# A streaming-encoder block on one core: when a merged row is squared, where one half of a gate is kept, and how the last norm is fed and cut

## The chip, the core and the metric

The kernel runs on one core of a Trainium2 chip. The metric is the time of one execution in microseconds (us), as the device reports it; lower is better. In the profile the engines are called PE (TensorE, with PEld for its loads of stationary weights), DVE (VectorE), ACT (ScalarE), POOL (GpSimd) and SP (SyncE, which here only issues DMAs). ACT and POOL issue some DMAs too, and each engine works through its own instructions strictly in program order.

## What is computed

One layer over a sequence of 1024 tokens with 1024 channels, in float32 at its edges:

```python
x = x + 0.5 * swiglu_ffn(rms_norm(x, ffn1_norm), ffn1_w_in, ffn1_w_out)
h = rms_norm(x, mix_norm)
q_a, k_a, v_a, q_i, k_i, w_i, u_s, q_m, gates = split(h @ w_in)
o_a = indexed_sparse_attention(q_a, k_a, v_a, q_i, k_i, w_i, rel_bias) @ w_o_a
y_s = gelu(s5_layer(u_s, ...))
glu_a, glu_b = split(y_s @ w_glu, 2)
o_b = glu_a * sigmoid(glu_b)
o_m = memory_attention(q_m, m_k, m_v) @ w_o_m
g = sigmoid(gates)                                   # three gates per channel
merged = g[:, :, 0] * o_a + g[:, :, 1] * o_b + g[:, :, 2] * o_m
x = x + merged @ w_out
x = x + 0.5 * swiglu_ffn(rms_norm(x, ffn2_norm), ffn2_w_in, ffn2_w_out)
x = rms_norm(x, final_norm)
```

The change touches the place where `merged` is formed, and the last `rms_norm`.

## The kernel before

**Layout.** Activations are kept transposed: 128 channels on the partitions, tokens along the free axis. A "row" is one such slab of 128 channels by 1024 tokens, so there are 8 rows (d = 0 to 7), and a row has two halves of 512 tokens. Each float32 operand of a matrix product is split into two float16 parts, high and low, and a product is three matmuls (high by high, high by low, low by high). Before a row can be an operand it is scaled by a power of two taken from its sum of squares.

**Order of the work.** The program is laid out by hand-written generators (threads) that a small planner interleaves: a cost model keeps a clock for each engine and decides which thread takes its next step, and after each step it issues, ahead of time, preparation of the weight blocks that come next (load, squares, scale, high part, low part), as long as its model says that ACT and DVE are less than 3 us behind PE. The planner only fixes the program order; on the chip each engine runs its list and waits on semaphores.

**The merging loop** (in `mixer`) has 16 steps, n = 2d + half. A step does 30 matmuls into four PSUM banks: `gb` (the GLU's second half), `ga` (its first half), `pm` (memory attention) and `po` (sparse attention); `ga` and `po` take turns in the two banks called mm. The other engines then merge. ACT evaluates `sb` = tanh(gb), `gc` = a scaled copy of ga, and `sm` = a scaled copy of pm; DVE multiplies them with each other and with the three gates, which come back from DRAM through a GpSimd DMA (`g_in`, 768 KB a step) into a ring of three places in the big buffer `xa`; POOL adds sb and sm. The last part of a step, `rest`, belongs to `po`, and is issued at the head of the next step: ACT copies po to the row's place `m` in `xa`, DVE multiplies it with its gate, POOL adds sb. `sb`, `sm` and `gc` come from one ring of four temporary places (`t2`).

When the second half of a row is done, `rest` also calls `w["m"].put(d, ...)`. That starts the row's split, in three parts: first ACT squares the row (with the sum); then, at the next `w["m"].more()`, DVE makes the scale by two operations on one column (and two more for the inverse), and ACT writes the high part; at the `more()` after that DVE writes the low part. A step calls `more()` twice, ahead of the loads of gates and after POOL's first add.

**After the loop** comes the product with `w_out` (`out_stage`). Its first weight block, `w["out"][0]`, is scaled by factors of the rows 0 to 5, so its scale can only be made when row 5 is split: a weighted sum on DVE (`wj`), a matmul with ones on PE, three or four small operations on DVE, and then high and low part of each of the six pieces on ACT and DVE. `w["out"][0].go(("split", 0))` at the end of the loop issues whatever the planner has not issued by then. Four output pieces run their part over rows 0 to 5 before rows 6 and 7 are needed.

**The end of the kernel.** The second FFN's output product (`out_stage` again) adds to `x`; `final` turns each finished piece back to tokens by channels with PE transposes (`turn`), multiplies it with the norm's weights `gb` (broadcast to all partitions, in a place of `xa` that the FFN's gate rows used), and with the last channel row works out the token's rstd and scales and stores the finished tokens. The last output piece (d = 7, second half) is cut into two pieces of 256 tokens, by `cut=(0, HT // 2, HT)`. `gb` is loaded by a DMA on ACT's queue just before this stage's loads of `x`.

Of the kernel before, what the change touches and what calls it, by code (L numbers as in the profile page):

```python
# [17 lines left out]
P = 128  # L18
S = 1024
D = 1024  # L20
ND = D // P
HT = 512
# [582 lines left out]
class Builder:  # L605
# [1605 lines left out]
    def mixer(self, w, xa, ss, xd_in, xd_out, after):  # L2211


        nc, tc, sched = self.nc, self.tc, self.sched
# [84 lines left out]
        heads = lambda t, half: lambda i, k: t[:, 4 * half:4 * half + 4, 2 * k + i]  # L2299
        gates, mt, xf = {}, {}, xa.rearrange("p k a h t -> p (k a h t)")  # L2300
        room = lambda i, n: xf[:, i * HT:(i + n) * HT].rearrange("p (j t) -> p j t", j=n)

        def g_in(n):
            if n < 2 * ND:
# [7 lines left out]
        for n in range(2 * ND):  # L2312
            d, half = divmod(n, 2)
            b = w["go"][d // 2]
            glu, wm, wa = b.segs
            c = (d % 2) * P
            yield from self.stream.begin(b)
            gb, ga = self.bank("lg"), self.mm()
            self.matmul3(gb, lambda i, k: glu.hl[:, i, k, 256 + c:256 + c + P], w["y"].x(half), 2)
            if late:  # L2320
                late.pop()()
            yield None
            self.matmul3(ga, lambda i, k: glu.hl[:, i, k, c:c + P], w["y"].x(half), 2)
            sb, sm, gc = self.t2("sb"), self.t2("sm"), self.t2("gc")
            nc.scalar.activation(sb, gb, AF.Tanh, scale=glu.inv)
            yield None
            w["m"].more()
            g_in(n + 2)
            ta, tg, tm = (gates[n][:, j] for j in range(3))
            pm, po = self.bank("ao"), self.mm()  # L2330
            self.matmul3(pm, lambda i, k: wm.hl[:, i, k, c:c + P], heads(qmS, half), 2)
            nc.scalar.activation(gc, ga, AF.Copy, scale=glu.inv)
            nc.vector.scalar_tensor_tensor(sb, sb, 1.0, gc, op0=OP.add, op1=OP.mult)
            nc.vector.scalar_tensor_tensor(sb, tg, 1.0, sb, op0=OP.add, op1=OP.mult)
            yield None
            self.matmul3(po, lambda i, k: wa.hl[:, i, k, c:c + P], heads(qS, half), 4, ks=range(2))
            nc.scalar.activation(sm, pm, AF.Copy, scale=wm.inv)
            nc.vector.scalar_tensor_tensor(sm, tm, 1.0, sm, op0=OP.add, op1=OP.mult)
            nc.gpsimd.tensor_tensor(sb, sb, sm, op=OP.add)
            w["m"].more()  # L2340
            yield None
            self.matmul3(po, lambda i, k: wa.hl[:, i, k, c:c + P], heads(qS, half), 4, ks=range(2, 4))
            self.stream.end(b)
            if half == 0:
                mt[d] = room(9 + 2 * (d % 3), 2)

            def rest(d=d, half=half, wa=wa, po=po, ta=ta, sb=sb):
                m = mt[d][:, half]
                nc.scalar.activation(m, po, AF.Copy, scale=wa.inv)
                nc.vector.scalar_tensor_tensor(m, ta, 1.0, m, op0=OP.add, op1=OP.mult)  # L2350
                nc.gpsimd.tensor_tensor(m, m, sb, op=OP.add)
                if half == 1:
                    w["m"].put(d, mt[d].rearrange("p h t -> p (h t)"))

            late.append(rest)
            yield None
        w["out"][0].go(("split", 0))
        late.pop()()
        self.stream.BACKLOG = 3
        nc.free.add(xa.tensor.name)  # L2360
        en.close()
        xo, F = after()
        pool = m3.enter_context(tc.tile_pool(name="xo4", bufs=1, side="right"))
        xo = xo + [pool.tile([P, HT], F32, name="xo4", tag=f"xo4{i}") for i in range(3)]
        xo = iter([xo[i % len(xo)] for i in range(2 * ND)])
# [54 lines left out]
def tile_hybrid_block(ctx, tc, x, mem, ffn1_norm, ffn1_w_in, ffn1_w_out, mix_norm, w_in, a_q_gain, a_k_gain, rel_bias,  # L2420
# [66 lines left out]
    def main():  # L2487
        yield from kb.ffn_in("1", pa, a1, g1, xa, before)
        for h in range(2):
            sched.add(kb.norm_split(xa, h, lambda h=h: kb.row_sums(ss[h]), 1, "2"), 0)  # L2490
        xo = lambda: pa.tile([P, 2, HT], F32, name="xo", tag="gt", bufs=2)[:, 0]
        yield from kb.out_stage(b1, g1, xo, xd[0], 1, 2, kb.keep_x("2", xa, ss, xd[1]))
        st.close()
        with ExitStack() as en:
            F = {}

            def after():
                pool = en.enter_context(tc.tile_pool(name="g3", bufs=1, reuse_waits="tile"))
                F["pool"], F["B12", 0] = pool, pool.tile([P, ND // 2, 2, HT // 2], F16, name="FB12", tag="wsum1")
                names = ("B11", "B21", "B22", "T1", "T2", "T3", "T4")  # L2500
                F["all"] = pool.tile([P, len(names), ND // 2, 2, HT], F16, name="F")
                for i, n in enumerate(names):
                    F[n] = F["all"][:, i]
                F["xo"] = [pool.tile([P, HT], F32, name="xo3", tag=f"xo3{i}") for i in range(4)]
                return F["xo"], F

            yield from kb.mixer(mw, xa, ss, xd[1], xd[2], after)
            nc.free.discard(xa.tensor.name)
            pool = en.enter_context(tc.tile_pool(name="g4", bufs=1, reuse_waits="tile"))
            F["B12", 1] = pool.tile([P, ND // 2, 2, HT // 2], F16, name="FB12", tag="H7")  # L2510
            tiles = xa.rearrange("p k a h t -> p (k a h t)").rearrange("p (i t) -> p i t", t=HT)
            n = {"post": 0, "gt": 0, "xo": 0}

            def ring(kind):
                n[kind] += 1
                i = n[kind] - 1
                if kind == "xo":
                    return F["xo"][i % 4]
                if kind == "gt":
                    i = 8 + 2 * (i % 2)  # L2520
                    return tiles[:, i:i + 2].rearrange("p i t -> p (i t)")
                return tiles[:, i % 8]

            def room(k):
                k %= chunks[0][1]
                if k > 8:
                    i = 12 + 2 * (k - 9)
                    return tiles[:, i:i + 2].rearrange("p i t -> p (i t)").bitcast(F16).rearrange("p (j t) -> p j t", j=2)
                return pool.tile([P, 2, S], F16, name="H", tag=f"H{k}")

            g2.room = room
            early = lambda f: pool.tile([P, 2 * HT], F32, name="early", tag=f"H{4 + f}")
            yield from kb.ffn_strassen("3", g2, a2, b2, F, ring, early, chunks, xd[2])
            gb = tiles[:, 8:10].rearrange("p i t -> p (i t)")
            nc.scalar.dma_start(gb, final_norm.to_broadcast([P, D]))
            xt = F["all"].rearrange("p n k j t -> p (n k j t)").bitcast(F32)[:, 0:S * D // P].rearrange("p (i n) -> p i n", n=D)
            done, between = kb.final(xt, ss, gb, out[0])
            yield from kb.out_stage(b2[-1], g2, lambda: ring("xo"), xd[2], 2, 2, done, 3, cut=(0, HT // 2, HT), between=between)
            between()

    sched.add(setup(), 1)
# [32 lines left out]
```

## Time and profile before

| | us |
|---|---|
| Time before, median of 3 runs (2272.67 to 2274.34) | 2273.84 |
| The profiled execution, its own time | 2275.79 |
| its span, first to last instruction | 2273.9 |
| PE busy | 2155.2 (95%) |
| DVE busy | 1353.6 (60%) |
| ACT busy | 1187.5 (52%) |
| POOL busy | 399.1 (18%) |

The profiled execution is 1.95 us above the median of the runs, and its time is 1.9 us above its span. Granted TensorE clock over the span: 0.98 of full. PE is busy nearly throughout, so the stretches in which it is not are where time can be won; the shares of the other engines are means over stages that are limited by different things.

### The profile page before, as it was taken

What the parts mean: (1) busy time and instruction counts of PE and PEld (TensorE: products, weight loads), DVE (VectorE), ACT (ScalarE), POOL (GpSimd) and SP (SyncE); (2) the same over time, 40 slices, a digit from 0 to 9 for tenths busy, and PEclk for the clock granted to TensorE, in tenths of its full rate; (3) what the DMA queues carried; (4) which work ended last, traced back from release to release, by engine and by line L of the source; (5) the groups of instructions that cost most, each with busy time, mean ns of one, the idle gap of its engine ahead of it and who ended that gap; (6) DMA issues with size and microseconds to landing.
All of it is one profiled execution on the core that took longest, in us unless ns stands there. A gap on an engine that the chain in (4) does not pass through costs nothing. (4 is left out here: it accounts for less than half of the span.)

```text
span 2273.9 us, 33537 instructions
## 1 busy us (share of the span) xinstructions
PE 2155.2 (95%) x12618; PEld 1154.3 (51%) x12622; DVE 1353.6 (60%) x3682; ACT 1187.5 (52%) x2368; POOL 399.1 (18%) x581
## 2 busy tenths in 40 slices
PE   7999999999999889979999999898999999999897
PEld 4555444444444556666566674344844444444344
DVE  6446853345555476768669876775746643566553
ACT  6543433344444488778877675544445432455421
POOL 1200130000000014302200005400434301344000
PEclk9999999999999999989999999998999999999998
DMA  6422231202222112123322123244011233112212
GB/s 222 121 86 79 58 102 56 63 26 84 88 88 84 47 32 68 45 64 121 124 68 76 48 69 129 101 146 133 2 55 56 70 125 121 47 56 63 88 54 93
DMA packets 204067, 185.20 MB, mean 81 GB/s; under 512 B 7376, under 2 KB 176528, under 8 KB 203264
## 3 DMA queue, kind: packets, MB, share of 16 engines
q1 hardware_dynamic: 185904, 135.84, 18.9%
q0 software_dynamic: 8272, 28.84, 3.9%
q10 hardware_dynamic: 9728, 18.38, 2.6%
q8 instruction: 99, 1.62, 0.3%
q14 instruction: 64, 0.52, 0.1%
HBM read 143.57 MB, written 40.50 MB: 81 GB/s over the span
## 5 line engine op out<-in xcount | busy, mean ns | idle before, releaser
L62 PEld LDWEIGHTS <-wh 128*128 128x128 f16 x8445 | 824.8, 99 | 954.9 <-issue 41.1
L62 PE MATMUL mm<-xa,wh 128*128 128x512 f16 x2382 | 541.1, 380 | 6.5 <-ACT xa L62 4.9
L62 PE MATMUL lg<-xa,wh 128*128 128x512 f16 x1080 | 244.2, 381 | 0.4 <-DVE xn L62 0.4
L62 ACT ACTIVATE junk<-wf 128x1024 f16<-128x1024 f32 (+3 forms) x292 | 193.9, 664 | 39.3 <-DMA wf<-in_ffn_w_in_dram 22.3
L62 PE MATMUL mm<-G,wh 128*128 128x512 f16 x960 | 210.5, 379 | 0.0
L62 DVE SCALAR_TENSOR_TENSOR wh<-wf,wsc,wh 128x1024 f16<-128x1024 f32 (+1 forms) x132 | 178.4, 1355 | 53.0 <-ACT wh L62 52.9
L62 PE MATMUL mm<-H,wh 128*128 128x512 f16 (+1 forms) x891 | 199.9, 381 | 8.1 <-ACT wh L62 7.8
L62 PE MATMUL lg<-F,wh 128*128 128x512 f16 (+1 forms) x900 | 180.7, 355 | 0.0
L62 ACT ACTIVATE wh<-wf,wrs 128x128 f16<-128x128 f32 (+2 forms) x304 | 112.9, 438 | 99.8 <-DVE wrs L62 92.8
L62 ACT ACTIVATE wh<-wf,wsc 128x1024 f16<-128x1024 f32 (+1 forms) x132 | 139.1, 1059 | 39.5 <-DVE wsc L62 26.0
L62 PE MATMUL mm<-wh,xa 128*128 128x256 f16 (+2 forms) x1152 | 129.5, 272 | 12.8 <-ACT us L62 6.7
L62 PE MATMUL mm<-F,wh 128*128 128x512 f16 (+1 forms) x672 | 130.9, 351 | 5.7 <-DVE xa L62 4.0
L62 PEld LDWEIGHTS <-xa 128*128 128x128 f16 x1152 | 108.2, 106 | 30.9 <-issue 14.3
L62 DVE SCALAR_TENSOR_TENSOR wh<-wf,wrs,wh 128x128 f16<-128x128 f32 (+2 forms) x304 | 111.8, 419 | 14.8 <-ACT wh L62 13.6
L62 DVE SCALAR_TENSOR_TENSOR gt<-lg,wsc,si 128x512 f32<-128x512 f32 x44 | 33.0, 750 | 130.1 <-PE lg L62 111.0
L62 PE MATMUL ao<-F,wh 128*128 128x512 f16 x456 | 104.6, 379 | 0.0
L62 ACT ACTIVATE junk<-wk,kathr 128x1024 f16<-128x1024 f32 (+2 forms) x96 | 99.5, 1036 | 8.7 <-POOL kathr L62 6.8
L62 POOL TENSOR_TENSOR xa<-hs,xa 128x512 f16<-128x512 f32 x16 | 19.9, 1249 | 478.0 <-ACT xa L62 478.0
L62 DVE SCALAR_TENSOR_TENSOR xo<-mm,wsc,xo 128x512 f32<-128x512 f32 x44 | 33.0, 750 | 112.0 <-PE mm L62 112.0
L62 POOL TENSOR_TENSOR xa<-xa 128x512 f32<-128x512 f32 (+1 forms) x40 | 58.0, 1452 | 173.9 <-ACT xa L62 168.1
L62 ACT ACTIVATE junk<-gt 128x1024 f16<-128x1024 f32 x22 | 23.2, 1056 | 116.5 <-DVE gt L62 116.5
L62 ACT ACTIVATE si<-mm,wsc 128x512 f32<-128x512 f32 x50 | 33.9, 677 | 92.7 <-PE mm L62 80.9
(510 smaller groups left out, 2993.4 us busy)
## 6 DMA issues: line engine op xcount, KB each, us to landing
wf<-in_ffn_w_in_dram SPq DMA_DIRECT2D x88, 512.0 KB, 4.8
xo<-xd ACTq DMA_DIRECT2D x64, 256.0 KB, 2.7
gd<-gt SPq DMA_DIRECT2D x48, 256.0 KB, 2.0
xa<-gd POOLq DMA_DIRECT2D x16, 768.0 KB, 5.1
wf<-in_ffn_w_out_dram SPq DMA_DIRECT2D x8, 1280.0 KB, 5.8
wf<-in_ffn_w_out_dram SPq DMA_DIRECT2D x7, 1408.0 KB, 6.1
wf<-in_w_in_dram SPq DMA_DIRECT2D x17, 512.0 KB, 4.8
xd<-xa SPq DMA_DIRECT2D x32, 256.0 KB, 2.4
```

The lines of the kernel that those rows point to most:

```text
L62: r = f(*a, **k)
```

## The change

Three edits, all in the order and the place of work that is done either way:

1. In the merging loop a finished row is not handed to `put` in `rest` but kept in a list, `ready`; it is taken from there after the second `more()` of the same step. Its square so stands behind this step's `sb`, `gc` and `sm` in ACT's order instead of ahead of them, and its scale, high and low part move into the following step. The last row is put after the loop, as before.
2. `gc` has a place of its own, the sixteenth slab of `xa`, which nothing else uses in this loop. The ring of four so holds `sb` and `sm` alone.
3. `gb` is loaded by GpSimd's DMA queue instead of ACT's, and the last output piece is no longer cut.

```diff
         room = lambda i, n: xf[:, i * HT:(i + n) * HT].rearrange("p (j t) -> p j t", j=n)
+        spare, ready = xf[:, 15 * HT:16 * HT], []
...
-            sb, sm, gc = self.t2("sb"), self.t2("sm"), self.t2("gc")
+            sb, sm, gc = self.t2("sb"), self.t2("sm"), spare
...
             nc.gpsimd.tensor_tensor(sb, sb, sm, op=OP.add)
             w["m"].more()
+            if ready:
+                w["m"].put(*ready.pop())
             yield None
...
                 if half == 1:
-                    w["m"].put(d, mt[d].rearrange("p h t -> p (h t)"))
+                    ready.append((d, mt[d].rearrange("p h t -> p (h t)")))
...
         late.pop()()
+        w["m"].put(*ready.pop())
...
-            nc.scalar.dma_start(gb, final_norm.to_broadcast([P, D]))
+            nc.gpsimd.dma_start(gb, final_norm.to_broadcast([P, D]))
...
-            yield from kb.out_stage(b2[-1], g2, lambda: ring("xo"), xd[2], 2, 2, done, 3, cut=(0, HT // 2, HT), between=between)
+            yield from kb.out_stage(b2[-1], g2, lambda: ring("xo"), xd[2], 2, 2, done, 3, between=between)
```

## Rows read from the trace of the kernel before

**Rows 1.** The page, busy time of each engine over the span (share, instructions).

```profile
PE 2155.2 (95%) x12618; PEld 1154.3 (51%) x12622; DVE 1353.6 (60%) x3682; ACT 1187.5 (52%) x2368; POOL 399.1 (18%) x581
```

**Rows 2.** Busy time by stage: the merging loop, and from its end to where PE runs without a break. Columns: stretch, its length, then busy us and instructions of PE, PEld, DVE, ACT, POOL, granted clock, DMA share, GB/s.

```profile
1357.60:1475.90 118.30, 105.35 (x490) 46.86 (x487) 81.86 (x143) 66.97 (x117) 57.34 (x43) 1.00 0.39 129
1475.90:1489.60 13.70, 10.04 (x38) 3.83 (x37) 9.95 (x25) 5.24 (x12) 3.97 (x3) 0.88 0.24 75
```

**Rows 3.** The waits in the merging loop, 1357.6 to 1475.9: who waited, for whom, us in total, times, the longest.

```profile
ACT junk L62 <- POOL xa L62: 31.5, 7, 6.1
DVE rsc L62 <- ACT junk L62: 14.3, 7, 2.7
DVE sb L62 <- ACT gc L62: 12.6, 8, 2.1
PE mm L62 <- ACT gc L62: 9.8, 6, 2.7
ACT sm L62 <- POOL sb L62: 8.7, 7, 1.8
```

**Rows 4.** The timeline around one row's square (row 1, step 4): start, duration, engine, operation, and the idle time before it with what ended it. `junk<-xa` is the square.

```profile
1387.92 1.27 POOL L62 TENSOR_TENSOR xa<-xa,sb 128x512 f32<-128x512 f32 x1 [0.72 <-DVE xa L62]
1389.22 1.06 ACT L62 ACTIVATE junk<-xa 128x1024 f16<-128x1024 f32 x1 [4.77 <-POOL xa L62]
1390.40 0.34 DVE L62 TENSOR_SCALAR rsc<-rsc 128x1 int32<-128x1 int32 x2 [2.65 <-ACT junk L62]
1390.85 1.14 ACT L62 ACTIVATE m<-xa,rsc 128x1024 f16<-128x1024 f32 x1
1391.89 0.67 ACT L62 ACTIVATE gc<-mm,wsc 128x512 f32<-128x512 f32 x1
1392.66 0.69 DVE L62 SCALAR_TENSOR_TENSOR sb<-sb,gc 128x512 f32<-128x512 f32 x1 [1.66 <-ACT gc L62]
```

**Rows 5.** The timeline of DVE and POOL where they run at the same time: three pairs, each a POOL add and the DVE instruction beside it.

```profile
1409.47 2.23 POOL L62 TENSOR_TENSOR sb<-sb,sm 128x512 f32<-128x512 f32 x1 [4.86 <-DVE sm L62]
1410.49 1.76 DVE L62 SCALAR_TENSOR_TENSOR xa<-xa 128x512 f32<-128x512 f32 x1
...
1417.82 1.26 POOL L62 TENSOR_TENSOR xa<-xa,sb 128x512 f32<-128x512 f32 x1 [0.69 <-DVE wsc L62]
1417.97 1.14 DVE L62 TENSOR_SCALAR wrs<-yi,wsc 128x2 f32<-128x2 f32 x1
...
1447.39 1.26 POOL L62 TENSOR_TENSOR sb<-sb,sm 128x512 f32<-128x512 f32 x1 [1.24 <-DVE wsc L62]
1447.40 0.15 DVE L62 TENSOR_SCALAR wsc<-wsc 128x1 int32<-128x1 int32 x1
```

**Rows 6.** The timeline: PE at the first two steps of the loop; then PE and POOL from the loop's end on (`mm<-m` are the first matmuls with w_out).

```profile
1357.61 1.46 PE L62 MATMUL lg<-y,wh 128*128 128x512 f16 x6
1364.09 1.46 PE L62 MATMUL lg<-y,wh 128*128 128x512 f16 x6
...
1475.94 1.24 PE L62 MATMUL mm<-m,wh 128*128 128x512 f16 x5
1481.24 7.90 PE L62 MATMUL mm<-m,wh 128*128 128x512 f16 x28 [2.85 <-DVE wh L62]
1483.12 1.26 POOL L62 TENSOR_TENSOR xa<-xa,sb 128x512 f32<-128x512 f32 x1 [2.22 <-DVE xa L62]
1489.57 1.45 PE L62 MATMUL mm<-m,wh 128*128 128x512 f16 x6 [0.42 <-DVE xo L62]
```

**Rows 7.** The timeline where the second FFN's last rows meet its output product (`xa<-in_final_norm_dram` is the load of gb), one stretch of busy time by stage after it, and the first use of gb.

```profile
2127.93 1.15 ACT L62 ACTIVATE xa<-xa,rsc 128x1024 f16<-128x1024 f32 x1 [0.41 <-DVE rsc L62]
2129.18 1.29 DVE L62 SCALAR_TENSOR_TENSOR xa<-xa,rsc 128x1024 f16<-128x1024 f32 x1 [0.97 <-ACT xa L62]
2130.49 0.34 ACTq L62 DMA_DIRECT2D xa<-in_final_norm_dram  x1
2132.41 2.74 PE L62 MATMUL mm<-H,wh 128*128 128x512 f16 x6 [6.52 <-ACT wh L62]
...
2130.60:2137.40 6.80, 4.99 (x13) 1.77 (x14) 4.63 (x19) 4.82 (x15) 0.00 (x0) 0.50 0.55 171
...
2153.26 0.68 DVE L62 TENSOR_TENSOR F<-lg,xa 128x512 f32<-128x512 f32 x1
```

**Rows 8.** The end of the kernel: the timeline of the uncut piece (7, first half) from its transposes on, of the merge of the piece before the cut one, and of the cut piece's second part; and busy time by stage (columns as in rows 2).

```profile
2243.02 0.60 PE L62 MATMUL lg<-ident,xn 128*128 128x128 f32 x4
2248.23 2.08 DVE L62 TENSOR_SCALAR F<-F,ny 128x1024 f32<-128x1024 f32 x3
2250.22 0.75 DVE L62 SCALAR_TENSOR_TENSOR xn<-mm,wsc,xo 128x512 f32<-128x512 f32 x1
2253.33 4.77 PE L62 MATMUL mm<-H,wh 128*128 128x256 f16 x27
2257.94 0.82 PE L62 MATMUL mm<-xa,wh 128*128 128x256 f16 x6
...
2253.30:2256.80 3.50, 3.50 (x19) 2.44 (x19) 0.56 (x2) 0.00 (x0) 0.00 (x0) 0.52 0.62 250
...
2249.50:2255.50 6.00, 4.70 (x32) 3.48 (x31) 3.32 (x7) 0.63 (x1) 0.00 (x0) 0.83 0.99 387
2272.20:2273.90 1.70, 0.00 (x0) 0.00 (x0) 0.00 (x0) 0.00 (x0) 0.00 (x0) 0.50 0.00 0
```

## The prediction

> **What bounds the kernel now.** I read the busy shares first: PE is busy 95% of the span [rows 1], so a change is worth what it takes from PE's pauses. Busy time by stage then says where they are. In the merging loop PE is busy 105.35 of 118.3 us, and in the 13.7 us behind it 10.04, at a clock of 0.88 [rows 2]. A step's 30 matmuls take 6.48 us, from the first step's start to the second's [rows 6], so 16 steps would take 103.7 us; the loop takes 118.3 [rows 6], 14.6 more. After it, 36 matmuls take from 1475.94 to 1489.57, 13.6 us [rows 6], where 36 x 6.48/30 = 7.8 would do: 5.8 more. So 20.4 us is the most that the first two edits can give.
>
> The waits of the loop come next. PE's main one is for ACT's copy `gc`, 9.8 us in 6 times [rows 3]. The timeline of one row shows why that copy is late [rows 4]: ACT stands still for 4.77 us before the square, because POOL's add is not done, and everything behind the square in ACT's order waits too. Seven rows cost ACT 31.5 us like this [rows 3]. DVE then waits for the square (14.3 us, 7 times) and for `gc` behind the high part (12.6 us, 8 times) [rows 3]. So the loop is a chain through all three engines, once per row: DVE, POOL's add, ACT's square, DVE's scale, ACT's high part and `gc`, DVE.
>
> DVE and POOL do not run side by side. A merge of 0.69 us [rows 4] takes 1.76 beside a POOL add, and that add 2.23 instead of 1.27 [rows 4, 5]: one waits until the other has finished. They must be counted as one resource, nearly as full as PE.
>
> **The change, part by part.** *The row taken later, and the place for gc.* Nothing is removed or added; 7 squares (1.06 us), 7 high parts and 7 low parts move. In the new order ACT has `sb`, `gc` and `sm` ahead of the square. `sm` can't be copied before 18 of the step's 30 matmuls are through, 3.9 us into the step, and takes 0.7; POOL's add needs a copy, a merge and itself from the step's start, 0.7 + 0.7 + 1.27 = 2.7 us. So with DVE less than 1.9 us behind, the square finds the add done. DVE's scale comes in the step after, again without a wait. What this saves is read from DVE's 14.3 us. Between the add's end (1387.92 + 1.27 = 1389.19) and DVE's start (1390.40) lie 1.2 us in which neither of the two runs [rows 4]; seven of these are 8.4 us, and they go in any case. The other 5.9 us (14.3 - 8.4) is time in which the add ran with DVE idle. It is won only if the add can run in another of DVE's pauses, and there is one: while ACT does high part and `gc`, 1.66 us [rows 4], long enough for an add of 1.27. So the loop's chain shortens by 8.4 to 14.3 us; I take the middle, 11.4.
>
> That needs one more thing. In the new order the scale's two operations come right behind the merge that releases the add. If they had to wait for the add, the high part would be late by 1.27 us per row. The rows say that they don't: an operation on two columns took 1.14 us beside an add, but one on a single column 0.15 [rows 5], and the scale is a single column [rows 4]. The Trainium skill's page "SBUF — State Buffer", section "Who interferes with whom", counts tensor_scalar among the operations that can take both of DVE's ports, and then the later of DVE and GpSimd is blocked for the other's whole instruction; its exclusive lock agrees with the 1.76 and 2.23 us of rows 5. Read for every tensor_scalar, that would block the scale and leave the first edit with 2.5 us; by the single column's 0.15 us it keeps its 11.4.
>
> The ring of four without `gc` ends ACT's wait of `sm` for POOL's add (8.7 us, 7 times [rows 3]), since a place is then used again two steps later, not one. ACT is not the bound, so I count it at nothing by itself: it is what lets DVE's lag stay off PE. The price of the own place is that `gc` waits for DVE's read of the step before, which comes 0.8 us behind `gc` [rows 4] and some 5 us before the next.
>
> *What the move delays.* Row 5 is split one step later, and with it `wj`, the matmul with ones and the six pieces of the first weight block of w_out. That block is already late: PE waits 2.85 us for its low parts [rows 6]. If the planner still gets these steps in before the loop ends, nothing is added; if they all come after it, I bound it by another wait of that size. Between 0 and 2.85 I take half, 1.4. First two edits: 11.4 - 1.4 = 10.0 us. The g_in DMA stays ahead of POOL's next add, and SP's weight loads keep their order.
>
> *gb by GpSimd's queue.* The load may only start when DVE has read the place's old row for its last low part, at 2129.18 + 1.29 = 2130.47, and ACT, whose own work ends at 2127.93 + 1.15 = 2129.08, stands in line for it until 2130.49 + 0.34 = 2130.83 [rows 7]. Behind it in ACT's order are two loads of x and the high parts for which PE waits 6.52 us [rows 7]. Without it they come 2130.83 - 2129.08 = 1.75 us sooner, and so does PE. POOL has no work left by then, so nothing stands behind the DMA there; gb is first used at 2153.26, 22 us later [rows 7]. The clock is 0.50 from 2130.6 to 2137.4 with PE busy 4.99 us of it [rows 7], a loss of 2.5 us. If the shorter pause spares that, the edit gives 4.2; if the slow stretch ends where it does now, half of the 1.75 is lost, 0.9. I take 1.75.
>
> *The last piece uncut.* Before, the second part's matmuls start at 2253.33 and end at 2257.94 + 0.82 = 2258.76, at a clock of 0.52 for the first 3.5 us [rows 8]. Uncut, `turn` of the piece before stands behind 18 of the 33 matmuls, at the same place in time as now, and 15 of 0.216 us follow: end at 2253.33 + 3.24 + 0.16 (what six matmuls' 1.46 us has over 6 x 0.216 [rows 6]) = 2256.7, or, with the clock at half for 3.4 us, 1.5 later, 2258.4. After PE's last matmul come now 2273.9 - 2258.76 = 15.1 us, with a wait of the second part's merge for the first part's chain on DVE. Uncut the chain is that of the piece (7, first half): merge 0.75 and two gaps of 0.05, from its transposes to its scaling 2248.23 - 2243.02 = 5.2, from there to the last byte of four tiles 2255.5 - 2248.23 = 7.3, and 1.7 from the last byte to the end [rows 8]: 15.05. The two tails are equal: a shorter chain is paid for by four tiles to store at once. So the edit gives 2258.76 less 2258.4 or 2256.7: 0.3 to 2.1, I take 1.2.
>
> **The sum**: 10.0 + 1.75 + 1.2 = 13 us, on the profiled execution 2275.79 - 13 = 2262.8, on the median of the runs 2273.84 - 13 = 2260.8.
>
> **The rivals.** *Only the square's wait goes.* DVE has work for every moment in which the add used to run alone, so the add blocks it there, and the late weights cost their full 2.85: 8.4 - 2.85 + 2.95 = 8.5, or 2265.3. For it: DVE and POOL are busy 81.86 and 57.34 us of 118.3 [rows 2]. Against: part of these is waiting for each other [rows 5].
>
> *The scale waits for the add* after all, 7 x 1.27 = 8.9 us: 13 - 8.9 = 4.1, or 2269.7. Against it stands the single column's 0.15 us [rows 5].
>
> *The change does not free ACT*: DVE lags so far that the add is no earlier ahead of the square than now; the last two edits alone give 2.95, or 2270.9. For it: the add behind the loop starts at 1483.12, 7.2 us after PE left it [rows 6].
>
> *Slower.* The first weights of w_out come a whole step later, 6.48 us, because row 5 does, and the loop is no shorter; PE stands still so long that its clock falls as it does in the other long pause, for 6.8 us at half [rows 7], 3.4 more. 9.9 - 2.95 = 6.9, or 2280.8. It decides from the point where PE's pause after the loop grows by more than the loop has given, plus 2.95. Against it: `go` issues these steps at the loop's end at the latest, and their chain is a few operations of under 1 us.
>
> *More*: all of DVE's 14.3, no late weights, both clocks kindly: 14.3 + 4.2 + 2.1 = 20.6, or 2253.2.
>
> **How the numbers follow.** A measurement of this kernel can tell some 0.2%, 4.5 us, from no change. Chances: forecast 0.50 (2256 to 2265), only the square's wait 0.20, the scale waits 0.08, ACT not freed 0.10, slower 0.07, more 0.05. Faster by over 4.5 us (below 2269.3) are the forecast, nine tenths of the second, half of the third, a fifth of the fourth, and the kindest: 0.50 + 0.18 + 0.04 + 0.02 + 0.05 = 0.79; slower 0.07; within, 0.14. The range goes from 2253, the kindest case, to 2272, past the case in which only the last two edits count; it leaves out the slower case and the edges.
>
> **What the changed profile would show.** Right: the wait of the square for POOL's add gone or under 5 us; PE's wait for `gc` gone; the loop near 108 us; 1.7 us less between the last FFN row and PE's first matmul of the last product; one scaling of four tiles at the very end, 15 us after PE's last matmul. Wrong: a pause of PE of over 5 us before the first matmuls with w_out; scale operations of over 1 us in the loop; DVE and POOL waiting for each other for as long as was saved; or the planner, which sees other times in its model, laying out a later stage differently.

## The result, and the profile after

The changed kernel takes 2261.03 us (median; 2257.67 to 2263.25), the kernel before 2274.09 beside it: a ratio of 0.9942, 95% interval 0.9925 to 0.9959, or 13.1 us. The forecast was 2260.8. The total came out as forecast; its terms did not, and the rest of this document is about them.

The profiled execution took 2263.25 us, with a span of 2261.5, 12.4 less than before. Times in the next table are landmarks on PE in the two profiled executions; each is the start of the same group of matmuls, or an end where it says so.

| landmark | before | after | gained so far |
|---|---|---|---|
| loop begins | 1357.61 | 1357.38 | 0.2 |
| loop ends, first matmuls with w_out | 1475.94 | 1466.05 | 9.9 |
| third unit of that product (the one that waits for `xo`) | 1489.57 | 1477.77 | 11.8 |
| end of that product's last matmul | 1567.28 | 1557.56 | 9.7 |
| last stage begins (its first `mm<-H`) | 2123.14 | 2115.97 | 7.2 |
| PE goes on after its pause there | 2132.41 | 2122.46 | 10.0 |
| transposes of the piece (7, first half) | 2243.02 | 2233.12 | 9.9 |
| end of the span | 2273.9 | 2261.5 | 12.4 |

So the loop gave 9.7 us, two more came behind it, and 4.6 of these 11.8 were given back before the last stage: 2.1 in the rest of the product with w_out and 2.5 in the second FFN. What the first two edits kept is 7.2 us, the pause gave 2.8 and the tail 2.5.

The loop in the changed kernel, busy time by stage (to compare with [rows 2]) and the waits (to compare with [rows 3]; the copy that was called `gc` is now an ACT operation into `xa`, because that is where its place lies):

```profile
1357.38:1466.05 108.67, 106.07 (x491) 47.56 (x489) 85.27 (x159) 70.85 (x126) 55.10 (x43) 0.98 0.42 142
...
ACT m L62 <- DVE rsc L62: 8.3, 6, 1.6
ACT junk L62 <- POOL xa L62: 6.8, 3, 3.1
PE ms L62 <- DVE wj L62: 2.4, 1, 2.4
```

The square's wait for POOL's add fell from 31.5 to 6.8 us, DVE's wait for the square and ACT's wait of `sm` for the add are gone from the list, and so is PE's wait for `gc`. ACT now waits for the scale ahead of the high part, 8.3 us in six times, but PE's only wait left in the list is the one for `wj`. Fifteen of the sixteen steps take 6.47 to 6.77 us. The fifteenth takes 10.73, and PE's timeline shows why (start, duration, idle time before with its releaser):

```profile
1453.97 0.16 PE L62 MATMUL ms<-wss,ones_b 128*128 128x1 bf16 x1 [2.37 <-DVE wj L62]
1453.99 2.35 PE L62 MATMUL ao<-qmS,wh 128*128 128x512 f16 x6
...
1454.50:1457.92 3.42, 3.42 (x11) 1.22 (x10) 3.35 (x12) 2.39 (x4) 0.73 (x1) 0.52 0.02 5
```

The matmul with ones for the first w_out block stands in PE's order ahead of the step's next matmuls, and its input `wj` is 2.4 us late. Behind it the granted clock is 0.52 for 3.4 us with PE busy all the time, which costs another 1.7 (six matmuls take 2.35 us instead of 1.46). In the run of the first two edits alone, below, the same wait of 2.4 us has no slow stretch behind it. DVE's order at that moment shows what `wj` was late for:

```profile
1447.18 1.09 DVE L62 TENSOR_TENSOR mj<-mi 128x1 f32<-128x1 f32 x1
...
1452.08 1.75 DVE L62 SCALAR_TENSOR_TENSOR xa<-xa 128x512 f32<-128x512 f32 x1
1453.75 0.15 DVE L62 SCALAR_TENSOR_TENSOR wj<-wrq,mj 128x6 f32<-128x6 f32 x1
```

Row 5's factor `mj` was done at 1448.27. Five merges and splits, among them one of 1.75 us beside a POOL add, stand between it and `wj` in DVE's order.

Behind the loop the pause of [rows 6] for the first weights is almost gone, 0.56 instead of 2.85 us, and another has come:

```profile
1469.79 4.92 PE L62 MATMUL mm<-m,wh 128*128 128x512 f16 x22 [0.56 <-DVE wh L62]
1472.17 1.06 ACT L62 ACTIVATE junk<-xa 128x1024 f16<-128x1024 f32 x1 [5.22 <-POOL xa L62]
1473.35 0.34 DVE L62 TENSOR_SCALAR rsc<-rsc 128x1 int32<-128x1 int32 x2 [2.62 <-ACT junk L62]
1474.98 1.28 DVE L62 SCALAR_TENSOR_TENSOR m<-xa,rsc,m 128x1024 f16<-128x1024 f32 x1 [1.03 <-ACT m L62]
1476.98 0.74 DVE L62 SCALAR_TENSOR_TENSOR xo<-mm,wsc,xo 128x512 f32<-128x512 f32 x1
1477.77 1.82 PE L62 MATMUL mm<-m,wh 128*128 128x512 f16 x5 [3.06 <-DVE xo L62]
```

This is the last row's chain through three engines: add, square, scale, high part, low part. DVE stands 2.62 and 1.03 us in it, and the `xo` merges that free PE's banks are queued behind; the first of them ends at 1477.72, and PE goes on. Before, PE was held up by the weights at this place and the same chain ended in its shadow (0.42 us left, [rows 6]). Now it is uncovered, 3.06 us, and the clock falls behind it (0.51 from 1478.40 to 1481.80). In the kernel before the clock had fallen earlier, behind the wait for the weights (0.88 over 13.7 us, [rows 2]). So the product only moves its pauses: from the loop's end to its last matmul it takes 91.3 us before and 91.5 after.

Behind it comes the second FFN. Busy time by stage from the product's last matmul to the last stage's first `mm<-H`, and the longest of PE's first pauses there, before and then after:

```profile
1567.28:2123.14 555.86, 534.65 (x2756) 271.12 (x2756) 313.85 (x532) 253.13 (x415) 184.49 (x124) 0.98 0.22 69
1582.84 0.16 PE L62 MATMUL ms<-wss,ones_b 128*128 128x1 bf16 x1 [4.15 <-ACT junk L62]
...
1557.56:2115.97 558.41, 534.52 (x2756) 270.38 (x2756) 314.50 (x533) 253.97 (x416) 184.69 (x125) 0.97 0.22 68
1573.81 0.16 PE L62 MATMUL ms<-wss,ones_b 128*128 128x1 bf16 x1 [5.75 <-ACT junk L62]
```

No edit touches this stage, and it has as many matmuls as before, but it takes 2.5 us longer. Its first pauses come to 12.5 us instead of 9.8. The planner has put the matmul with ones that waits for ACT's squares of a weight block behind 24 of the stage's matmuls; before, it stood behind 48.

The pause where the second FFN's rows meet its output product, to compare with [rows 7]; the first line is the same work of ACT on the weights in the kernel before:

```profile
2131.85 2.10 ACT L62 ACTIVATE wh<-wf,wrs 128x256 f16<-128x256 f32 x5 [2.77 <-issue]
...
2120.76 1.15 ACT L62 ACTIVATE xa<-xa,rsc 128x1024 f16<-128x1024 f32 x1 [0.41 <-DVE rsc L62]
2120.76 0.81 ACTq L62 DMA_DIRECT2D xo<-xd  x2
2121.90 2.10 ACT L62 ACTIVATE wh<-wf,wrs 128x256 f16<-128x256 f32 x5
2122.46 0.60 PE L62 MATMUL mm<-H,wh 128*128 128x512 f16 x2 [3.74 <-ACT wh L62]
2123.61 0.61 POOL L62 DMA_DIRECT2D xa<-in_final_norm_dram  x1 [4.44 <-DVE xa L62]
```

POOL now waits for the old row's last reader, and nothing stands behind it. The two loads of `x` are issued while ACT's high part runs and take no time of their own: ACT turns to the weights as soon as its high part ends, where it stood for 2.77 us before.

The last piece, uncut, to compare with [rows 8]:

```profile
2243.43 2.10 PE L62 MATMUL mm<-H,wh 128*128 128x512 f16 x9
2245.37 1.46 PE L62 MATMUL mm<-xa,wh 128*128 128x512 f16 x6
...
2243.40:2249.80 6.40, 4.05 (x21) 1.81 (x20) 0.92 (x2) 1.22 (x7) 0.00 (x0) 0.99 0.33 134
```

PE's last matmul ends at 2246.83, and 14.7 us follow (before 15.1). The clock is full throughout the piece.

### The profile page after: what moved, and what is told of

Its sections match the earlier page's. It is cut to its first block, busy times and chain, and to the rows that moved or that the text cites. A ratio compares the mean times of both kernels' runs of the same rounds, so it can differ in the third digit from the quotient of the medians.

```text
span 2261.5 us, 33474 instructions
## 1 busy us (share of the span) xinstructions
PE 2153.0 (95%) x12585; PEld 1150.1 (51%) x12589; DVE 1351.2 (60%) x3669; ACT 1187.9 (53%) x2367; POOL 397.0 (18%) x582
## 5 line engine op out<-in xcount | busy, mean ns | idle before, releaser
L62 PE MATMUL mm<-H,wh 128*128 128x512 f16 x864 | 197.4, 383 | 6.0 <-ACT wh L62 5.0
L62 PE MATMUL mm<-F,wh 128*128 128x512 f16 (+1 forms) x672 | 130.4, 349 | 6.7 <-ACT F L62 2.8
L62 DVE SCALAR_TENSOR_TENSOR wh<-wf,wrs,wh 128x128 f16<-128x128 f32 (+2 forms) x304 | 113.5, 425 | 13.3 <-ACT wh L62 12.1
L62 PE MATMUL ao<-F,wh 128*128 128x512 f16 x456 | 104.6, 379 | 0.0
L62 ACT ACTIVATE xa<-mm,wsc 128x512 f32<-128x512 f32 x51 | 34.8, 682 | 103.7 <-PE mm L62 102.6
```

What stands on the lines that cost most here:

```text
L62: r = f(*a, **k)
```

## The experiments

Each run's ratio is to the kernel before, measured beside it, whose median was 2273.3 us in the first group of four, 2274.0 in the second and 2272.93 in the third.

**The change taken apart.** The first edit alone, the kernel before with the row taken later:

```diff
-                    w["m"].put(d, mt[d]...)       # in rest
+                    ready.append((d, mt[d]...))
...
             w["m"].more()
+            if ready:
+                w["m"].put(*ready.pop())
```

> Only the row taken later; gc stays in the ring of four. Theory: it is the square ahead of sb, gc and sm in ACT's order that holds PE, so the merging loop shortens from 118.3 to about 110 us, ACT's wait of the square for POOL falls from 31.5 to under 8 us, and the time falls by 5 to 6 us. Rival: the ring is what couples ACT to POOL, so that the wait only moves from the square to the copy sm: the loop stays above 115 us and the time within 3 us of before.

2267.78 us, ratio 0.9978 (0.9968 to 0.9987). The second edit alone:

```diff
-            sb, sm, gc = self.t2("sb"), self.t2("sm"), self.t2("gc")
+            sb, sm, gc = self.t2("sb"), self.t2("sm"), spare
```

> Only the own place for gc; the row is squared where it was. Theory: ACT's wait of sm for POOL's add (8.7 us) goes, but the square still blocks ACT once a row, so the loop stays at 116 to 118 us and the time within 2 us of before. Rival (the ring is the coupling): the loop falls to about 110 us and the time by 5 us or more.

2279.05 us, ratio 1.0024 (1.0014 to 1.0034): slower. Both together, without the third edit:

> The two edits of the loop together, without those of the last stage. Theory: the loop as in the changed kernel, 108.7 us, and the time 7 to 8 us below before, since the gain of the loop (9.7) is partly given back behind it (clock, the wait for the residual). If the parts add up, that is the sum of the two kernels with one part each. Rival: the last stage's edits carry the gain and this gives under 4 us.

2265.27 us, ratio 0.9967 (0.9954 to 0.9979), 8.0 below the kernel before, as the theory had it. The loops of the three, the row later, the own place, and both (busy time by stage, and waits of the square and of PE):

```profile
1356.20:1467.27 111.07, 106.27 (x490) 47.40 (x488) 86.64 (x159) 71.36 (x126) 57.21 (x43) 0.98 0.41 139
ACT junk L62 <- POOL xa L62: 8.3, 5, 1.9
PE mm L62 <- ACT gc L62: 2.3, 3, 0.9
```

```profile
1357.51:1480.17 122.66, 108.23 (x489) 47.84 (x487) 85.21 (x149) 69.83 (x124) 57.65 (x43) 0.97 0.38 126
ACT junk L62 <- POOL xa L62: 32.9, 7, 6.0
PE mm L62 <- ACT xa L62: 11.3, 6, 4.1
```

```profile
1356.11:1463.52 107.41, 104.56 (x490) 47.12 (x488) 84.17 (x157) 69.67 (x124) 55.30 (x43) 1.00 0.43 144
PE ms L62 <- DVE wj L62: 2.4, 1, 2.4
```

The first edit takes the square's wait away, 8.3 us instead of 31.5, and that is 7.3 us of the loop. The own place shortens the loop by 3.7 us more on top of it (111.07 to 107.41), of which 1.7 are PE's own matmuls at another clock (busy 106.27 and 104.56 us); by the runs it is 2.5 us (2267.78 to 2265.27), and the two intervals overlap. Alone it makes the loop 4.3 us longer, 2.9 of them again PE's own matmuls (108.23 for 105.35 us), and the product behind it 4.6 (96.0 for 91.3). That had not been expected by either theory. The timeline of the worst step with the own place alone:

```profile
1421.14 1.06 ACT L62 ACTIVATE junk<-xa 128x1024 f16<-128x1024 f32 x1 [6.00 <-POOL xa L62]
1423.51 0.75 DVE L62 SCALAR_TENSOR_TENSOR wh<-wf,wsc,wh 128x512 f16<-128x512 f32 x1 [3.82 <-ACT wh L62]
1424.18 0.34 DVE L62 TENSOR_SCALAR rsc<-rsc 128x1 int32<-128x1 int32 x2
...
1426.33 1.44 PE L62 MATMUL mm<-y,wh 128*128 128x512 f16 x3 [4.11 <-ACT xa L62]
```

The square still blocks ACT, here for 6.0 us. The planner has put a weight's high and low part (`wh`) between square and scale. DVE waits 3.82 us for that high part, with the scale behind it, so high part of the row, `gc` and PE all follow later, and PE stands for 4.11 us. In this step the planner's order is a bad one on the chip; how much of the whole loss comes in this way was not measured.

The third edit's first half alone, `gb` by GpSimd's queue in the kernel before:

```diff
-            nc.scalar.dma_start(gb, final_norm.to_broadcast([P, D]))
+            nc.gpsimd.dma_start(gb, final_norm.to_broadcast([P, D]))
```

> Only gb's load moved to GpSimd's queue. Theory: PE's first matmul with the late weights comes 2.8 us sooner (it was 2132.41 - 2123.14 = 9.3 us after the first matmul of this stage, and should be 6.5), because ACT's two loads of x go out under its high part and the weights' high parts follow at once; the time falls by 2.8 us, or by 1.75 if the two loads still take ACT's time as the prediction had it. Rival: the load from GpSimd is late or held up by VectorE, and gb's first use waits: no gain.

2268.64 us, ratio 0.998 (0.9971 to 0.9989). From the stage's first matmul to where PE goes on it is 6.24 us instead of 9.27, 3.0 us less, and 3.0 less at the transposes too, so the clock gave nothing beyond the pause.

Its second half alone, the last piece uncut (the `cut` argument left out):

> The kernel before with its last output piece uncut and nothing else changed. Prediction's term: 0.3 to 2.1 us faster (1.2), with 15 us from PE's last matmul to the end, as before. After the changed kernel's trace (tail 14.7 us, the granted clock full until two thirds of the piece) I now expect the kind end, 2.1 to 2.5 us: 2271 where before is 2273.3. Rival: the gain seen in the changed kernel is only that the slow stretch of the clock fell elsewhere there; then this one still shows a clock near 0.5 in the last piece's first matmuls, and the gain is 0.3 to 0.6 us. Other rival, four tiles to store at once cost more than the cut did: the tail over 16 us, and no gain.

2273.5 us, ratio 0.9999 (0.9991 to 1.0008): no difference. PE at the start of the last piece, and the clock in it:

```profile
2253.57 3.79 PE L62 MATMUL mm<-H,wh 128*128 128x512 f16 x9
...
2253.57:2257.00 3.43, 3.43 (x11) 1.26 (x11) 0.16 (x1) 0.00 (x0) 0.00 (x0) 0.51 0.58 236
```

The same nine matmuls that took 2.10 us in the changed kernel take 3.79 here, at half the clock, although the groups around them are the same and start at the same distances. The rival holds: the 2.5 us of the changed kernel's tail are the clock's 1.7 and 0.8 else. (In this run's profile the stretch from the transposes to the end is 29.9 us instead of 30.9; its runs show no gain.) The parts add up: 8.0 us for the first two edits (2273.3 - 2265.27; by the interval of the ratio 4.8 to 10.5), 4.7 for `gb` (2273.3 - 2268.64; 2.5 to 6.6), 0.5 for the cut (2274.0 - 2273.5; -1.8 to 2.0), 13.2 where 13.1 was measured. With intervals as wide as these, so close an agreement is luck.

**The wait for wj.** Row 5 alone given to its split as early as before, the rest as changed:

```diff
-                    ready.append((d, mt[d]...))
+                    row = d, mt[d]...
+                    w["m"].put(*row) if d == 5 else ready.append(row)
```

> The changed kernel, but row 5 alone is given to its split in rest, as before, so that the factors of the first weight block of w_out are known a step earlier; all other rows stay late. Theory: PE's wait of 2.4 us for wj in step 14 and the slow clock behind it (3.4 us at half, 1.7 us lost) come from row 5's later split and are gone; step 14 takes 6.5 to 7 instead of 10.7 us, and the loop 105 to 106 instead of 108.7. The price is one square in step 12 that waits some 4 us for POOL's add. In all 0 to 4 us faster than the changed kernel, 2257 to 2261. Rival: the wait is given by the planner's place for the matmul with ones, not by row 5: PE waits as long in another step, and the loop stays at 108 to 109 us.

2258.89 us, ratio 0.9937 (0.9924 to 0.9949), no different from the changed kernel's 0.9942. The pause did not go with the earlier row:

```profile
1444.32 2.72 PE L62 MATMUL mm<-y,wh 128*128 128x512 f16 x6 [3.05 <-ACT xa L62]
1451.67 0.16 PE L62 MATMUL ms<-wss,ones_b 128*128 128x1 bf16 x1 [1.64 <-DVE wj L62]
```

The rival holds in the main: the planner puts the matmul with ones 18 matmuls sooner when the row is sooner, PE waits for `wj` all the same, and the blocked square costs PE 3.05 us at `gc` again. The loop is 111.3 us, worse than either expectation; behind it the weights are in time, and from the loop's beginning to the end of the product it is 201.4 us, 1.2 more than in the changed kernel. The second FFN then takes 553.8 instead of 558.4 us. So the time lies where the theory had it, but not for its reason.

The matmul with ones later, nothing else:

```diff
+        w["out"][0].LATE = 4.0
         self.stream.BACKLOG = 3
```

(`LATE` is how long after its time by the model the planner leaves a block's scale alone.)

> The changed kernel, but the planner issues the scale of the first weight block of w_out (weighted sum on DVE and PE's matmul with ones) later, behind more of PE's work. Theory: the wait of 2.4 us is there because PE's instruction stands too early in its order, and what needs its result has slack; later it costs nothing: the loop 105 to 106 us, PE's first matmuls with w_out without a longer pause, 2257 to 2260. Rival: the weights behind it are needed as soon as they are made; the wait only moves behind the loop, as a pause of 2 to 5 us at the first matmuls with w_out, and the time is that of the changed kernel or up to 2 us more (2261 to 2263).

2248.42 us, ratio 0.9886 (0.9871 to 0.9901), 12.6 us below the changed kernel and 26 below the kernel before: the fastest of all kernels run here. The loop, the pauses behind it, and the second FFN (from the product's last matmul to the last stage, as above):

```profile
1358.30:1463.93 105.63, 104.40 (x492) 47.25 (x490) 81.55 (x154) 68.43 (x120) 56.66 (x43) 1.00 0.45 146
...
1468.67 7.64 PE L62 MATMUL mm<-m,wh 128*128 128x512 f16 x28 [2.85 <-DVE wh L62]
1477.44 4.04 PE L62 MATMUL mm<-m,wh 128*128 128x512 f16 x18 [1.13 <-DVE xo L62]
...
1556.04:2103.35 547.31, 530.83 (x2757) 269.08 (x2757) 311.77 (x530) 253.85 (x415) 181.52 (x123) 0.99 0.22 70
```

The matmul with ones stands 18 matmuls further on. No wait for `wj` in the loop, every step at 6.47 to 6.77 us (but for 1.1 us at the loop's very end), the clock at full. The wait moves behind the loop, as the rival had it (2.85 us), but the row's chain is covered by it again (1.13 instead of 3.06). From the loop's beginning to the end of the product with w_out this is 2.5 us of gain (197.7 for 200.2 us). By the profiles the rest, 11.1 us, lies in the second FFN (547.3 for 558.4 us) and was not foreseen: PE's waits there come to 16.5 us instead of 24.0, and its own matmuls take 3.7 us less, at a clock of 0.99 for 0.97. The planner, whose clocks now stand differently, has put the matmul with ones that waits for ACT's squares behind 120 of this stage's matmuls, where it stood behind 24, and it waits 3.48 us instead of 5.75.

The same, twice as late:

```diff
-        w["out"][0].LATE = 4.0
+        w["out"][0].LATE = 8.0
```

> The changed kernel with the scale of the first w_out block issued twice as late as in the run that gave 2248.4 us. If that gain hangs on the place in which the scale is issued, there is a slope: no wait for wj in the loop (105 to 106 us), but PE's pause at the first matmuls with w_out grows from 1.1 and 2.9 to some 6 us in all, 2250 to 2253. Rival: two thirds of the gain are an accident of the order of the second FFN's first steps; if that order falls back to the one of the changed kernel, the time is 2256 to 2260 with the same loop.

2258.23 us, ratio 0.9929 (0.9912 to 0.9947). The rival's number, but not its reason, and the six runs lie far apart (2248.63 to 2261.25). The loop is as good (106.0 us), and the second FFN keeps the better order (547.7 us), so what is lost against 4.0 lies elsewhere: PE waits 4.1 us for `wj` of the next block in the product with w_out (`PE ms <- DVE wj`, 4.1, once), the clock there is 0.83 for the first 20 us, and the product takes 98.7 us instead of 92.1; the last stage, from its first matmul to PE's last, takes 133.9 instead of 130.4, with the same waits at a lower clock. So 4.0 is better in the median than both 0 and 8.0, and the gain is not one mechanism's.

In the kernel before the same line (4.0):

> The kernel before, only with the scale of the first w_out block issued later. There PE waited 0.4 us for wj in the loop. If the late scale is worth something only because the changed kernel knows row 5 a step later, nothing is won here: loop 118 us, up to 1 us more behind it, 2273 to 2276. Rival: most of the 12.6 us that it gave the changed kernel come from another order of the second FFN's first steps, where PE stood for 12.5 us in pauses (before: 9.8) and then for 8.1; if that order comes here too, 2264 to 2268.

2274.27 us, ratio 1.0003 (0.9995 to 1.0012): nothing, as expected, and the second FFN does not take the better order (553.9 us; before 555.9). PE's wait for `gc` is still there (10.3 us in the loop), and the one for `wj` was small.

**POOL in the chain.** The changed kernel with both adds of the merge on VectorE:

```diff
-            nc.gpsimd.tensor_tensor(sb, sb, sm, op=OP.add)
+            nc.vector.tensor_tensor(sb, sb, sm, op=OP.add)
...
-                nc.gpsimd.tensor_tensor(m, m, sb, op=OP.add)
+                nc.vector.tensor_tensor(m, m, sb, op=OP.add)
```

> The changed kernel, but both adds of the merge are made by VectorE instead of GpSimd; same arithmetic. It measures whether the two engines count as one resource in the loop. If they do (a merge of 0.69 us takes 1.76 beside an add of 1.26, and that add 2.23): 32 adds of about 0.69 us replace 32 of 1.26 in the joint time, VectorE's busy time rises from 85 to at most 100 us (22 us of adds, less the waiting that is counted in its 85), and the loop stays within 1 us of 108.7 or becomes shorter, by up to 3; the time 2258 to 2262. If they run side by side apart from the few stretches seen, VectorE gets 22 us more, over 105 us of a loop of 108.7, PE waits for its merges in several steps, and the loop becomes 3 to 8 us longer: 2264 to 2269.

2253.9 us, ratio 0.9914 (0.9901 to 0.9926), 7.1 below the changed kernel. The busy times over the span and DVE's merge `xa<-xa` in the loop (count, busy us, mean ns, idle us before), first of the changed kernel, then of this run, and this run's loop:

```profile
PE 2153.0 (95%) x12585; PEld 1150.1 (51%) x12589; DVE 1351.2 (60%) x3669; ACT 1187.9 (53%) x2367; POOL 397.0 (18%) x582
...
L62 DVE SCALAR_TENSOR_TENSOR xa<-xa 128x512 f32<-128x512 f32 x15 | 17.3, 1154 | 6.6 <-ACT xa L62 6.6
```

```profile
PE 2143.9 (95%) x12589; PEld 1143.8 (51%) x12589; DVE 1351.9 (60%) x3701; ACT 1189.3 (53%) x2367; POOL 348.2 (15%) x550
...
L62 DVE SCALAR_TENSOR_TENSOR xa<-xa 128x512 f32<-128x512 f32 x15 | 10.3, 686 | 2.6 <-ACT xa L62 2.6
...
1355.60:1462.90 107.30, 104.46 (x490) 46.84 (x488) 83.57 (x178) 69.93 (x120) 9.87 (x13) 1.00 0.43 144
```

VectorE has 32 instructions more, 22 us of adds at 0.69 each, and is busy 0.7 us longer over the whole span; in the loop even less than before (83.6 for 85.3 us, where some weight work fell outside). So some 21 us of its busy time in the changed kernel were waits for POOL inside its own instructions: the merge `xa<-xa` falls from 1.15 to 0.69 us in the mean. That is the theory in which the two count as one resource, though the time is below its 2258 to 2262: by the profiles 4.5 us are won up to the end of the product with w_out, and 4.7 more in the second FFN (553.7 for 558.4 us), which is the planner's order again. In the loop PE no longer waits for `wj`, behind it no longer for `xo` (for `wj` 0.8 us, for the first weights 2.2), and the clock is full in the 20 us behind the loop. One step of 10.0 us is left in the loop, for a weight block whose high part PE waits for 1.5 us and what follows from it.

Both improvements together, `LATE = 4.0` and the adds on VectorE:

> The changed kernel with both: the scale of the first w_out block issued later, and both adds of the merge on VectorE. Alone they took 2248.4 and 2253.9 us. If each removes a wait of its own (the one PE's wait for wj and the layout behind it, the other POOL from the merge's chain), the loop comes to the 104 to 105 us of PE's own work, the third unit's wait behind it falls under 2 us, and the time is 2242 to 2246. Rival: both buy the same thing, a VectorE that is less late at the end of the loop; then 2247 to 2250, no better than the first alone.

2258.61 us, ratio 0.9938 (0.9926 to 0.9951), worse than either alone. The loop is that of the adds on VectorE alone (107.3 us): with VectorE in time for `wj`, a later place for it has nothing to give. Behind it the order of the w_out blocks differs: between 40 and 80 us after the loop PE has pauses of 3.7 us in all, the larger ones for ACT's squares and high parts of weights, where the adds alone have none; the product takes 94.7 us instead of 88.4. Why the planner's order there is a worse one stays open.

The adds on VectorE in the kernel before:

> The kernel before, only with both adds of the merge on VectorE instead of GpSimd. It asks what made the square wait: GpSimd's part of the chain, or the square's place in ScalarE's order. If the hand-over to GpSimd and the time in which VectorE and GpSimd exclude each other were the cost, 32 adds of 1.26 us become 32 of 0.69 (18 us less of joint time): the loop falls from 118.3 to 107 to 111 us, 2263 to 2267. If the square's place is the cost, ScalarE still stands in front of it until VectorE's last merge of the row is done; its waits stay over 20 us in all, the loop over 114, and the time 2270 to 2274.

2271.54 us, ratio 0.9996 (0.9988 to 1.0005). The time is that of the second theory, the trace is not quite (waits in the loop, which takes 118.1 us):

```profile
ACT junk L62 <- DVE xa L62: 16.8, 7, 4.1
PE ms L62 <- DVE wj L62: 6.6, 2, 3.5
PE mm L62 <- ACT gc L62: 2.2, 3, 1.1
```

The square blocks ACT half as long, and PE's wait for `gc` falls from 9.8 to 2.2 us, as the first theory would have it. The loop is no shorter, because PE waits 6.6 us for `wj` instead, where it was 1.6 before. So POOL's part and the square's place both made the row late. With POOL's part alone taken away nothing is won; what this run does not tell is what it would give with the matmul with ones at a better place.

## Why the prediction came out

**The loop's chain: 8.4 to 14.3 us, 11.4 taken.** It gave about 13.7: the loop fell by 9.66 us although it now holds the wait of 2.37 for `wj` and some 1.7 of slow clock (9.66 + 2.37 + 1.7). The loop without these is 104.6 us, against 103.7 of bare matmuls. The run of the first two edits alone gives 13.3 (118.3 - 107.4 + 2.4). The loop now runs at PE's own pace, so the chain became shorter by at least this much, and the 11.4 was too little. The step that had left the 5.9 us in doubt was right about the pause in which the add can run, and too careful: the add of the next fence ends at 1409.76, and DVE stands until 1411.13 for ACT's high part and copy. The reason named, DVE's wait between POOL's add and the scale, is the one the trace shows gone, and the run of the first edit alone, 7.3 us with the square's wait at 8.3, bears it out.

**The scale beside the add.** It did not wait. The two operations of `rsc` take 0.33 or 0.34 us for all seven rows in the loop, three times with a POOL add already running; one of them with that add:

```profile
1408.44 1.32 POOL L62 TENSOR_TENSOR xa<-xa,sb 128x512 f32<-128x512 f32 x1 [1.30 <-DVE xa L62]
1408.94 0.33 DVE L62 TENSOR_SCALAR rsc<-rsc 128x1 int32<-128x1 int32 x2
...
1409.37 0.41 DVE L62 TENSOR_TENSOR mj<-mi 128x1 f32<-128x1 f32 x1
```

The operation behind them with two inputs, also on one column, did wait (0.41 us here, 1.09 beside a longer rest of an add, 0.16 beside none), which held up nothing that PE waited for. So that rival falls. The Trainium skill's page "SBUF — State Buffer", section "Who interferes with whom", has for the second kind that an operation with two inputs in SBUF contends with a GpSimd operation that reads SBUF; the 0.41 and 1.09 us agree. For tensor_scalar it names the two-port form alone; the 0.33 us show that on one column it was not blocked.

**Own place: "nothing by itself".** This step failed. Alone the own place makes the loop 4.3 us longer and the kernel slower (2279.05 us). With the row taken later the loop is 3.7 us shorter, of which 1.7 are the clock, and the runs give 2.5 us that they can't tell from nothing. ACT was "not the bound", but it stands in the chain for `gc`, for which PE waits. And the step took the order for given, where the planner lays it out anew after every edit.

**The late weights: 0 to 2.85 us, 1.4 taken.** Mis-sized and misplaced. The pause for the first weights shrank, from 2.85 to 0.56. In its place PE waits for `wj` inside the loop, 2.4 us and 1.7 of clock; and behind the loop for `xo`, 3.06 us and 1.7 of clock, where 0.42 was. The prediction had looked at the chain of the first block's weights only, and not at what would be late next when that one is not: the last row's chain, which the same wait had covered. In sum the loop holds 4.1 us of it and the product takes 0.2 us longer, 4.3 where 1.4 was taken. The two errors nearly cancel: up to the end of the product with w_out the first two edits give 9.5 us (209.7 before, 200.2 after), where 10.0 was forecast.

**The second FFN: put at nothing.** It takes 2.5 us longer. The run of the first edit alone, that of the first two and the changed kernel have it alike (558.4, 557.8 and 558.4 us; before 555.9). The sum has no term for it, though the planner's laying out a later stage differently stands among the signs of being wrong. So the first two edits kept 7.2 us by the profile and 8.0 by the runs.

**gb: 0.9 to 4.2 us, 1.75 taken.** Mechanism right, size short: 2.8 us here, 3.0 alone in the profile, 4.7 by its runs (2.5 to 6.6). The step counted ACT's stand in line, 1.75 us, and left the two loads of `x` behind it in the path as though they cost ACT time as before. They are another 1.0 us of ACT's 2.77 before the weights; once nothing stands ahead of them they are issued beside the high part and no longer count.

**Uncut: 0.3 to 2.1 us, 1.2 taken.** The two ends were the two clocks, and both clocks came: 2.5 us in the changed kernel with the clock at full; alone, with the clock at half, 0.9 us in the profile and no measurable difference by the runs. The tails are near equal as worked out (14.7 and 14.6 against 15.1). (The working says 1.5 us for 3.4 us at half clock, which lose 1.7; its 2258.4 goes by the 1.7.) So the edit itself is worth 0.8 or 0.9 us in either profile, and 1.7 of the changed kernel's 2.5 are a clock that fell elsewhere, which no edit aimed at.

So the mechanism of the loop was right, and the sum was right by luck, by errors that cancel: 2.3 us too little for the chain against 2.9 too little for the late weights, and 2.5 not counted in the second FFN against 2.3 too little for the last stage, 1.7 of these the clock. Of the rivals, "only the square's wait goes" named 2265.3 us, which is what the first two edits take without the third; but its reason, adds that block DVE where they used to run alone, did not come in that measure: DVE's merges `xa<-xa`, with their waiting, take 1.15 us in the mean, before 1.47, while `mj` rises from 0.16 to 0.64. "The change does not free ACT" falls with the square's wait, 31.5 to 6.8 us (a little over the 5 named as a sign of being right). "Slower" was seen in one part, the own place alone, and not by that rival's way: PE's pause for the first weights shrank in the changed kernel.

## What to carry to other kernels

When a wait is taken away, list what ends next at the same place: a chain that was hidden by the old wait comes out as soon as it goes. Where a planner orders the program, each edit is also a new order, and two edits that each gain may give less together than either alone (2248 and 2254 us alone, 2259 together, 2261 without both); so measure the parts and the whole, and look for the pauses far from the edit. An instruction of a full engine that waits for a small result should stand behind work that is ready, not ahead of it: moving one matmul of 0.16 us later took its wait out of the loop in the fastest kernel here. That kernel won most of its time in a stage that no edit touched, so such a gain has to be measured; the working shown here does not find it.

## What the runs showed of the hardware

VectorE did 22 us more work and was busy 0.7 us more: the busy time of VectorE beside GpSimd was in part waiting, and read as work it says too much.

Two DMA issues on ACT's queue that had nothing to wait for, 0.81 us in all, began together with a high part of 1.15 us and did not lengthen it. In the kernel before, the issue that had to wait held up ACT's own next operations [rows 7].

The granted clock at a given group of matmuls differs between programs that are the same there: the last piece's nine matmuls took 2.10 us in one and 3.79 in the other. A gain of under 2 us at a stage's edge is not told from one profiled execution.
